# Samples and a norm row by DMA, and a new order from the out-projection to the up-projection

## The chip, the cores and the metric

The kernel runs on one core of a Trainium2 chip. The metric is the device time of one launch in microseconds. Of three runs of the kernel before, the median is 1061.47 us (1061.19 to 1062.1).

## What is computed

One layer of a hybrid decoder: 1,024 prompt tokens and 32 sample tokens (8 sequences of 4) of width 1,024, in float32.

```python
h = rms_norm(x, g_mix_pre) * (1 + sc1) + sh1
proj = h @ w_in
...
glu = a_c * jax.nn.sigmoid(b_c)
conv_c, new_cconv = causal_dwconv(glu, past_cconv, cconv_w)
y_c = jax.nn.silu(layer_norm(conv_c + cconv_b, cln_g, cln_b))
mix = jnp.concatenate([y_a, y_b, y_c], axis=-1) @ w_out
x = x + gt1 * rms_norm(mix, g_mix_post)

h = rms_norm(x, g_ffn_pre) * (1 + sc2) + sh2
up = h @ w_up
up_c, new_ffn = causal_dwconv(up, past_ffn, ffn_conv_w)
gate, val = jnp.split(up_c, 2, axis=-1)
ff = (jax.nn.silu(gate) * val) @ w_down
x = x + gt2 * rms_norm(ff, g_ffn_post)
```

`gate` and `val` have 2,816 columns each, 22 blocks of 128. A sample token's convolution takes the two last up-projected rows of its own sequence, so its 32 columns stand apart from the prompt's.

## The kernel before

Matmuls are made from two parts of each operand: a rounded one, `hi` (a cast on ACT), and the rest, `lo` (a subtraction on DVE, `sub_to`, L927). Three matmuls, hi by hi, hi by lo and lo by hi, make one product.

**Out-projection** (`mm2`, L833). Token tiles 0, 1 and 2 go first, together, with k-tiles in the order 2, 3, 4, 1, 0, 5, 6, 7; then tiles 3 to 8, tile 8 being the 32 samples. While k-tiles 3 and 4 run, the LayerNorm of the convolution's output is finished: `ln_rstd` (L442) makes 1,056 inverse deviations on POOL, three DMAs lay them as rows, three matmuls with K = 1 (`ln_bc`, L449) spread each third over the 128 partitions in PSUM, and `ln_apply` (L454, DVE) multiplies by them. `proj` (L607) is a small matmul of the pooling group; it takes its PSUM room from the same ring of two tiles (`psb`) as `ln_bc`. The w_out tiles `w` are loaded right behind the three row DMAs in SP's queue.

**From out-projection to up-projection.** Each token tile runs a chain: gate and residual (`gt`, `res`), second norm (`sq2`, `rs` on POOL, `xn2`), transposes on PE (`tr`, L897) and modulation (`mod`). The results of two neighbouring token tiles are combined into the operands of a scheme with seven products instead of eight (`t13`, `t24`, `t_hi`, `t_lo`).

**Up-projection** (`prod`, L1218). For each of 22 blocks of columns there are seven products (numbers 1 to 7) of 12 matmuls 128x512. Operands on the weights' side are the loaded `raw` and `rawb` and their sums (`s_sum`, `s_hi`, `s_lo`, tiles `s`, `sh`, `sl`). `snap` (ACT, L1223) copies a partial result from PSUM, and `c11`, `c22`, `c12`, `c21` (L1233, DVE, and L1239) add parts into `fext`, the convolution's input. Products 1 and 2 of blocks 0 and 1 run before tile 8 of the tokens is ready; then block 0 goes on with 6, 5, 7, 3, 4.

**Samples.** `smp` (L1253) multiplies the samples against each block, leaving them transposed in PSUM, in four parts. `smp_ev` copies this 128x128 with ACT (L1258); `smp_t` (L1262) turns it and adds pairs of parts on PE, by a matmul with the 0/1 matrix `sel`; `smp_out` (L1266, ACT) copies the result into `fext`.

**What sets the order.** PE, DVE, ACT and SP run in program order, and that order is written by hand: `at(time, f, args)` puts a call on a list, and `play` runs the list sorted by the time. The times serve the sorting alone; an instruction starts when its engine reaches it and its operands are there. Each block's operands are then taken from PSUM and the pools in that order, so that a wait in one place holds all behind it on the same engine.

Of the kernel before, what the change touches and what calls it, by code (L numbers as in the profile page):

```python
# [50 lines left out]
def body(ctx: ExitStack, tc: tile.TileContext, a, o):  # L51
# [17 lines left out]
    one1 = lnp.tile([P, P], F32, name="one1")  # L69
# [11 lines left out]
    dve.memset(one1, 1.0)  # L81
# [9 lines left out]
    gd = tc.dram_tile([9, 2048], F32, name="gd")  # L91

# [855 lines left out]
    def t24(i):  # L948
        r0, r1 = h2_of(i - 1), h2_of(i)
        sub_to(r1[:, 4:8], r1[:, 4:8], r0[:, 0:4])  # L950
        sub_to(r0[:, 4:8], r0[:, 4:8], r1[:, 4:8])

    def t_hi(i):
        act.copy(ycol(0, i), h2_of(i))

    def t_lo(i):
        sub_to(ycol(1, i), h2_of(i), ycol(0, i).bitcast(F32))
# [4 lines left out]
    def chain(i, e, tt):  # L962
        at(e, sq1, i)
        at(e + 1.1, rs, i)
        at(e + 1.2, gt, i)
        at(e + 2.4, res, i)
        at(e + 3.7, sq2, i)
        at(e + 4.8, rs, i)
        at(e + 5.5, xn2, i)
        at(tt, tr, i, 0)  # L970
        at(tt, tr, i, 1)
        at(tt + 0.7, mod, i, 0)
        at(tt + 1.1, mod, i, 1)
        at(tt + 2.5, h2_hi, i)
        if i % 2:
            at(tt + 2.5, t13, i)
            at(tt + 3.0, h2_lo, i)
            at(tt + 3.6, t24, i)
            for n, j in enumerate((i, i - 1)):
                at(tt + 4.6 + 1.1 * n, t_hi, j)  # L980
                at(tt + 5.7 + 1.2 * n, t_lo, j)
        else:
            at(tt + 3.5, h2_lo, i)

    def chain_s(e):
        for dt, f in ((0, sq1), (2.2, rs), (2.4, gt), (3.7, res), (4.9, sq2), (6.0, rs), (6.8, xn2)):
            at(e + dt, f, 8)
        for q in range(2):
            at(e + 11.74, tr, 8, q)
            at(e + 12.4 + 0.1 * q, mod, 8, q)  # L990
# [105 lines left out]
    for n, i in enumerate(order):  # L1096
# [7 lines left out]
        if i == 8:  # L1104
            at(t - 2.99, gate_s)
            chain_s(t + 2.0)
        else:
            te = max(t, te + 7.0)
            chain(i, te, te + 9.0)
# [3 lines left out]
    fs = {p: tc.dram_tile([FT // 2, P, 512], F32, name=f"fs{p}") for p in range(1, 8)}  # L1113
    U = {}
# [16 lines left out]
    def open_b():  # L1131
# [6 lines left out]
        U["sel"] = pools["p3b"].tile([P, 2, 32], F32, name="sel")  # L1138
        iv = ident.rearrange("p (a b n) -> p a b n", a=2, n=32)
        dve.tensor_tensor(out=U["sel"], in0=iv[:, :, 0], in1=iv[:, :, 1], op=ALU.add)  # L1140
# [25 lines left out]
    def s_sum(i, p):  # L1166
        ra, rb = U["ra", i], U["rb", i]
        a11, a12, a21, a22 = ra[:, 0:512], ra[:, 512:1024], rb[:, 0:512], rb[:, 512:1024]
        if p == 5:
            t, t2 = (pools["p3"].tile([P, 512], F32, name="s1", bufs=2) for _ in range(2))  # L1170
            U["s", i] = {5: t, 7: a21, 6: t2, 3: a12, 4: a22}
            dve.tensor_tensor(out=t, in0=a21, in1=a22, op=ALU.add)
        elif p == 7:
            sub_to(a21, a11, a21)
        elif p == 6:
            sub_to(U["s", i][6], U["s", i][5], a11)
        elif p == 3:
            sub_to(a12, a12, U["s", i][6])
# [30 lines left out]
    def prod(i, p):  # L1209
# [5 lines left out]
        for k in range(4):  # L1215
# [5 lines left out]
    def snap(i, n):  # L1221
        t = pools["p3" if n == "a" else "p3b"].tile([P, 512], F32, name=f"sn{n}", bufs=1)
        act.copy(t, x_of(i)[:, 0])  # L1223
        U["sn", n, i] = t
# [101 lines left out]
    DP, DS = 2.75, 1.6  # L1326
# [7 lines left out]
    at(t8 + 14.5, open_z)  # L1334
    at(t8 + 14.51, open_b)
    for i in range(2):
        t1 = t8 + 2 * DP * i
        at(t8 - 5.0 + 2.2 * i, a_hi, i)
        at(t8 - 3.9 + 2.2 * i, a_lo, i)
        at(t1, prod, i, 1)  # L1340
        at(t1 + DP, prod, i, 2)
        at(t1 + DP + 0.1, snap, i, "a")
        at(t8 + (6.1 if i == 0 else 14.6), c11, i)
# [9 lines left out]
    def sample(i, t, t1=None, t2=None):  # L1353
# [3 lines left out]
        at(t + DS, smp_ev, i)  # L1357
        at(t1 - 0.01, smp_t, i)
# [3 lines left out]
    for i in range(FT):  # L1362
        if i == 0:
            for p, ts, th, tl in ((5, 5.0, 6.1, 9.2), (6, 5.1, 6.0, 6.9), (7, 15.6, 15.7, 16.3), (3, 15.8, 16.8, 17.5), (4, 0, 12.0, 14.7)):
                if p != 4:
                    at(t8 + ts, s_sum, 0, p)
                at(t8 + th, s_hi, 0, p)
                at(t8 + tl, s_lo, 0, p)
            sample(0, b + DP + 0.9, b + 3 * DP + 2 * DS)
            sample(1, b + 2 * DP + DS + 0.9, b + 4 * DP + 2 * DS, b + 5 * DP + 2 * DS + 7.0)  # L1370
            seq = [(prod, 0, 6), (DS + 0.9,), (prod, 0, 5), (DS,), (prod, 0, 7), (prod, 0, 3), (prod, 0, 4)]
# [8 lines left out]
        for f, *args in seq:  # L1380
# [9 lines left out]
            j, p = args  # L1390
# [5 lines left out]
            elif p == 6:  # L1396
                at(done + (0 if j else 0.8), snap, j, "b")
            elif p == 5:
                at(done, snap, j, "c")
                if j:  # L1400
                    at(done + 0.8, c22, j)
            elif p == 7 and j == 0:
# [7 lines left out]
        if i == 0:  # L1410
            tg, tv = t - 1.0, t + 0.8
# [369 lines left out]
```

## Time and profile before

| | us |
|---|---|
| median of three runs | 1061.47 |
| the profiled execution | 1063.64 |
| its span | 1061.8 |
| PE busy | 1030.5 (97%) |
| DVE busy | 825.0 (78%) |
| ACT busy | 466.6 (44%) |
| POOL busy | 38.2 (4%) |

The profiled execution is 2.17 us above the median, and 1.84 us of it lie outside the span. TensorE's mean granted clock over it is 0.992 of full speed. The parts of the page go from the whole to the single instruction: busy shares of the engines, the span in slices, groups of instructions by line, DMA. A list of PE's waits tells which operand ended each, and a timeline gives start and length of single instructions. Matmuls overlap in the pipeline: a 128x512 is shown 0.39 us long while the next starts 0.23 us later, so distances are read from start to start.

### The profile page before, as it was taken

To read this page: it belongs to the slowest core of one execution; us is meant where nothing else is said; L and a number is where in the kernel's file an instruction comes from. 1 tells how busy PE (TensorE), PEld (TensorE's weight loads), DVE (VectorE), ACT (ScalarE), POOL (GpSimd) and SP (SyncE) were. 2 spreads that over 40 slices of the span, in tenths; PEclk is the share of its full clock that TensorE was granted. 3 is DMA by queue.
4 is the path that set the end of the run, shared out by engine and by line. 5 is a ranking of instruction groups with operands and counts; after the bars stand their busy time and mean duration, and the time that the engine had idled before them with its cause. 6 is when DMAs were issued, how large, how long until landed. Compare 5 with 4: busy or idle time off the path is not lost. (4 is left out here: it accounts for less than half of the span.)

```text
span 1061.8 us, 15512 instructions
## 1 busy us (share of the span) xinstructions
PE 1030.5 (97%) x6094; PEld 864.8 (81%) x6094; DVE 825.0 (78%) x1142; ACT 466.6 (44%) x835; POOL 38.2 (4%) x56
## 2 busy tenths in 40 slices
PE   5999999999999989999999999999999999999997
PEld 4999989997687668888888888888888787778885
DVE  5688898978547788888788788778878764987584
ACT  6331111115747745445454444544545464335551
POOL 3000000001011100000000000000000000020100
PEclk9999999999999989999999999999999999999999
DMA  8776652211512413323314223322323694325272
GB/s 334 262 228 194 193 185 88 63 41 17 184 43 99 156 54 99 109 64 127 110 60 129 91 79 115 104 80 92 114 74 110 228 412 179 109 73 161 90 267 100
DMA packets 68050, 141.10 MB, mean 133 GB/s; under 512 B 17156, under 2 KB 28676, under 8 KB 64904
## 3 DMA queue, kind: packets, MB, share of 16 engines
q1 hardware_dynamic: 66632, 135.77, 39.0%
q10 hardware_dynamic: 1344, 4.33, 1.0%
q8 instruction: 48, 0.79, 0.3%
q14 instruction: 26, 0.21, 0.1%
HBM read 110.18 MB, written 29.90 MB: 132 GB/s over the span
## 5 line engine op out<-in xcount | busy, mean ns | idle before, releaser
L1280 DVE SCALAR_TENSOR_TENSOR facc<-fext,par,facc 128x1072 f32<-128x1072 f32 x88 | 117.2, 1332 | 14.2 <-ACT facc L1273 12.7
L535 DVE SCALAR_TENSOR_TENSOR yb<-cext,par,yb 128x1024 f32<-128x1024 f32 x90 | 111.9, 1278 | 0.8
L279 PE MATMUL psa<-hh,whi 128*128 128x352 f32 x372 | 82.0, 328 | 0.0
L279 PE MATMUL psa<-hh,wlo 128*128 128x352 f32 x372 | 80.2, 323 | 0.0
L1532 PE MATMUL psd<-whi 128*128 128x512 f32 x204 | 80.1, 393 | 0.0
L279 PE MATMUL psa<-hl,whi 128*128 128x352 f32 x372 | 80.1, 323 | 0.0
L1532 PE MATMUL psd<-whi,wlo 128*128 128x512 f32 x204 | 79.6, 390 | 0.1
L1532 PE MATMUL psd<-wlo,whi 128*128 128x512 f32 x204 | 79.5, 390 | 0.1
L1513 ACT CAST whi<-fa 128x512 fp32r<-128x512 f32 x73 | 45.3, 621 | 70.9 <-PE psb L1532 24.6
L927 DVE TENSOR_TENSOR wlo<-fa,whi 128x512 fp32r<-128x512 f32 x73 | 49.9, 684 | 31.0 <-ACT whi L1513 31.0
L1218 PE MATMUL psc<-hh,sh 128*128 128x512 f32 x176 | 69.7, 396 | 2.8 <-DVE fext L1233 2.8
L1218 PE MATMUL psb<-hh,sh 128*128 128x512 f32 x176 | 71.3, 405 | 0.0
L1218 PE MATMUL psc<-hl,sh 128*128 128x512 f32 x176 | 69.6, 396 | 0.9 <-DVE hl L927 0.9
L1218 PE MATMUL psc<-hh,sl 128*128 128x512 f32 x176 | 69.4, 395 | 0.0
L1218 PE MATMUL psb<-hh,sl 128*128 128x512 f32 x176 | 68.8, 391 | 0.0
L1218 PE MATMUL psc<-bh,whi 128*128 128x512 f32 x176 | 68.6, 390 | 0.0
L1218 PE MATMUL psc<-bh,wlo 128*128 128x512 f32 x176 | 68.5, 389 | 0.0
L1218 PE MATMUL psc<-bl,whi 128*128 128x512 f32 x176 | 68.5, 389 | 0.0
L1218 PE MATMUL psb<-hl,sh 128*128 128x512 f32 x176 | 68.5, 389 | 0.0
L279 PEld LDWEIGHTS psa<-hh,whi 128*128 128x128 f32 x372 | 62.8, 189 | 6.4 <-issue 4.1
L279 PEld LDWEIGHTS psa<-hh,wlo 128*128 128x128 f32 x372 | 63.8, 188 | 0.0
L279 PEld LDWEIGHTS psa<-hl,whi 128*128 128x128 f32 x372 | 63.1, 188 | 0.0
(270 smaller groups left out, 2318.0 us busy)
## 6 DMA issues: line engine op xcount, KB each, us to landing
fa<-fs SPq DMA_DIRECT2D x73, 256.0 KB, 3.8
adaw<-in_ada SPq DMA_DIRECT2D x16, 1024.0 KB, 7.5
raw<-in_w_up SPq DMA_DIRECT2D x22, 512.0 KB, 3.6
rawb<-in_w_up SPq DMA_DIRECT2D x22, 512.0 KB, 3.7
fs<-facc SPq DMA_DIRECT2D x44, 256.0 KB, 2.5
b<-in_w_down SPq DMA_DIRECT2D x18, 512.0 KB, 7.3
fs<-whi SPq DMA_DIRECT2D x33, 256.0 KB, 2.3
adaw<-in_adag SPq DMA_DIRECT2D x8, 1024.0 KB, 7.1
```

Of the source, the lines that this page charges most:

```text
L279: pe.matmul(ps[:, c, 0:CW], lhsT=wt[:, k, :], rhs=h[:, k, c * CW:(c + 1) * CW], start=(k == 0 and n == 0), stop=(k == KT - 1 and n == 2))
L535: dve.scalar_tensor_tensor(out=y[:, 0:NPR], in0=e[:, k:k + NPR], scalar=par[:, off + k:off + k + 1], in1=y[:, 0:NPR], op0=ALU.mult, op1=AL ...
L927: dve.tensor_tensor(out=out, in0=x, in1=y, op=ALU.subtract)
L1218: pe.matmul(out, lhsT=w[:, ks], rhs=h(k), start=(p in (1, 2, 7) and k == 0 and n == 0), stop=(k == 3 and n == 2), skip_group_check=True)
L1280: dve.scalar_tensor_tensor(out=acc[:, 0:1072], in0=e[:, k:k + 1072], scalar=par[:, wo + k:wo + k + 1], in1=acc[:, 0:1072], op0=ALU.mult, o ...
L1513: act.copy(hi[:, 0:512], R[n, "raw"])
L1532: pe.matmul(ps, lhsT=s[:, cs], rhs=w, start=(first and m == 0), stop=(j == HK - 1 and m == 2), skip_group_check=True)
```

## The change

There are three parts.

1. **Norm row.** `ln_bc`, its matrix of ones and the three row DMAs go. `ln_rstd` stores the 1,056 values to DRAM (`rsd`) by one DMA, and a second DMA reads them back to all 128 partitions (540 KB) into a `zc` tile; `ln_apply` multiplies by that tile instead of by PSUM.
2. **Samples.** `smp_t` and `sel` go. `smp_ev` becomes a DVE transpose of 32x32 parts from PSUM, with a DMA that stores the 64 KB to DRAM (`smpd`). `smp_ld` is new: four DMAs of 32 partitions by 4 by 32 values (512 pieces of 128 bytes in all) bring it back as `smq`. `smp_out` becomes a DVE addition of two parts of 32 columns. This holds for all 22 blocks.
3. **The transition.** Tables `FIRST`, `SECOND` and `THIRD` fix the order of the last token tiles' chains and block 0's weights. Block 0's products run 6, 7, 5 (three of four k), then tile 8's transposes, the last k of 5, both samples' `smp`, 3, 4. `t24` falls into `t2` and `t4`, `t_hi` and `t_lo` into halves. Some results get other rooms: `t2` of tile 7, the sums 7 and 3 of block 0, one `snap` and tile 8's transposes. The weights of the blocks after are loaded and split at other times.

The core of the diff:

```diff
 def ln_rstd():
...
         pool.tensor_tensor(out=rt, in0=vt, in1=nhalf[0:96, :], op=ALU.pow)
-        for c in range(3):
-            sync.dma_start(rows[32 * c:32 * c + 1, :], rt[32 * c:32 * c + 32, :])
-
-    def ln_bc(c):
-        rw = slice(32 * c, 32 * c + 1)
-        ln["r", c] = psb()
-        pe.matmul(ln["r", c][:, 0:CW], lhsT=one1[rw, :], rhs=rows[rw, :], start=True, stop=True,
-                  tile_position=(32 * c, 0))
+        sync.dma_start(rsd.rearrange("o (q n) -> (o q) n", n=11), rt)
+        ln["r"] = zc_tile()[:, 0:T]
+        sync.dma_start(ln["r"], rsd.broadcast_to([P, T]))
...
     def tr(i, q):
         rows = tile_rows(i)
-        pt = psb()
-        pv = pt.rearrange("p (k n) -> p k n", n=P)[:, :, 0:rows]
+        if i < 8:
+            pv = psb().rearrange("p (k n) -> p k n", n=P)
+        else:
+            pv = U["s"][:, 256 + P * q:256 + P * q + P].rearrange("p (k n) -> p k n", n=rows)
...
-    def t24(i):
...
+    def t2(i):
         r0, r1 = h2_of(i - 1), h2_of(i)
+        st[i, "t2"] = r1[:, 4:8] if i < 7 else st[i, "t"][:, 0:512].rearrange("p (k n) -> p k n", n=P)
+        sub_to(st[i, "t2"], r1[:, 4:8], r0[:, 0:4])
+
+    def t4(i):
+        r0 = h2_of(i - 1)
+        sub_to(r0[:, 4:8], r0[:, 4:8], st[i, "t2"])
...
+    def t_hi(i, r=slice(0, KT)):
+        act.copy(ycol(0, i)[:, r], t_src(i, r))
...
+        elif p == 7 and i == 0:
+            t = U["s", i][7] = stream.tile([P, 1024], F32R, name="whi").bitcast(F32)[:, 0:512]
+            sub_to(t, a11, a21)
...
-    def prod(i, p):
+    def prod(i, p, k0=0, k1=4):
...
     def smp_ev(i):
         t = pools["p3"].tile([P, P], F32, name="smp", bufs=2)
-        act.copy(t, U["s"][:, P * (i % 2):P * (i % 2) + P])
-        U["smp", i] = t
-
-    def smp_t(i):
-        pe.matmul(U["s"][:, 256:320], lhsT=U["smp", i], rhs=U["sel"].rearrange("p a n -> p (a n)"), start=True, stop=True)
+        dve.transpose(out=t, in_=U["s"][:, P * (i % 2):P * (i % 2) + P])
+        sync.dma_start(smpd[i], t)
+
+    def smp_ld(i):
+        u = U["smp", i] = pools["p3"].tile([P, P], F32, name="smq", bufs=2)
+        for j in range(4):
+            sync.dma_start(u[32 * j:32 * j + 32].rearrange("m (q t) -> m q t", t=32),
+                           smpd[i].rearrange("(q m) (j t) -> j m q t", q=4, j=4)[j])
 
     def smp_out(i, v):
-        e = e_of(i, v)
-        act.copy(ext_parts(e, 2)[2], U["s"][:, 256 + 32 * v:288 + 32 * v].rearrange("p (s t) -> p s t", t=ST))
+        e, u = e_of(i, v), U["smp", i].rearrange("p (q s t) -> p q s t", q=4, t=ST)
+        dve.tensor_tensor(out=ext_parts(e, 2)[2], in0=u[:, 2 * v], in1=u[:, 2 * v + 1], op=ALU.add)
         act.copy(ext_state(e, 2), U["fst"][:, i + FT * v, 1:9, :])
...
+    FIRST = [(s_sum, 0, 5), (t2, 7), (s_sum, 0, 6), (t_hi, 7, HI), (s_hi, 0, 6), (t_lo, 7, HI), (snap, 0, "a"), (s_lo, 0, 6),
+             (c11, 0), (s_sum, 0, 7), (t_hi, 7, LO), (s_hi, 0, 7), (t_lo, 7, LO), (s_lo, 0, 7), (gt, 8), (res, 8), (t_hi, 6, LO),
...
+    for n, (f, *args) in enumerate(FIRST):
+        at(b - 0.5 + 0.01 * n, f, *args)
...
         at(t, smp, i)
-        at(t + DS, smp_ev, i)
-        at(t1 - 0.01, smp_t, i)
+        if i:
+            at(t + DS + 0.05, smp_ev, i)
+        at(t + DS + 4.0, smp_ld, i)
         at(t1 + 0.6, smp_out, i, 0)
...
-            seq = [(prod, 0, 6), (DS + 0.9,), (prod, 0, 5), (DS,), (prod, 0, 7), (prod, 0, 3), (prod, 0, 4)]
+            seq = [(prod, 0, 6), (prod, 0, 7), (prod, 0, 5, 0, 3), (2 * DS,), (prod, 0, 3), (prod, 0, 4)]
+            at(b + 2.8 * DP, prod, 0, 5, 3, 4)
```

**DVE, around the first addition into `fext` (`c11` of block 0).** Here `px` are the tokens' operands, `s`, `sl` the weights' sums and their lo parts. Before:

```order
270 L1172 TENSOR_TENSOR s_3394<-rawb 128x512
271 L927 TENSOR_TENSOR s_3395<-s_3394,raw 128x512
272 L927 TENSOR_TENSOR bl<-px,bh 128x4x128
273 L882 SCALAR_TENSOR_TENSOR px<-px,rs 32x1024
274 L927 TENSOR_TENSOR px<-px 128x512 x2
275 L1233 TENSOR_TENSOR fext_3343<-psc,sna 128x4x128
276 L927 TENSOR_TENSOR sl<-s_3395,sh 128x512
277 L927 TENSOR_TENSOR hl<-px,hh 128x8x128
```

After:

```order
268 L1173 TENSOR_TENSOR s_3411<-rawb 128x512
269 L923 TENSOR_TENSOR pt<-px 128x512
270 L923 TENSOR_TENSOR s_3412<-s_3411,raw 128x512
271 L923 TENSOR_TENSOR hl<-pt,hh 128x4x128
272 L923 TENSOR_TENSOR sl<-s_3412,sh 128x512
273 L1243 TENSOR_TENSOR fext_3335<-psc,sna 128x4x128
274 L923 TENSOR_TENSOR whi<-raw,rawb 128x512
275 L923 TENSOR_TENSOR hl<-px,hh 128x4x128
276 L923 TENSOR_TENSOR sl<-whi,sh 128x512
```

The addition into `fext` no longer stands behind the scaling of tile 8 (the 32x1024 row), nor behind the two `px` subtractions after it; of those only the one into `pt` is left ahead, and one half of `hl` with it. Tile 8's own steps come later.

**SP's queue, from the first `rawb` loads to the second block of weights.** Before:

```order
57 L1151 DMA rawb<-in_w_up 128x1024 x2
58 L1137 DMA fst<-in_st_f 128x792
59 L1147 DMA raw<-in_w_up 128x1024
60 L1151 DMA rawb<-in_w_up 128x1024
61 L1147 DMA raw<-in_w_up 128x1024
```

After:

```order
59 L1141 DMA fst<-in_st_f 128x792
60 L1270 DMA smpd<-smp 128x128 x2
61 L1152 DMA rawb<-in_w_up 128x1024
62 L1148 DMA raw<-in_w_up 128x1024
63 L1275 DMA smq<-smpd 32x4x32 x8
64 L1148 DMA raw<-in_w_up 128x1024
65 L1270 DMA smpd<-smp 128x128
```

Stores and loads of the samples now stand between the weights' loads: two stores, then a `rawb` and a `raw` of 512 KB each, then the eight loads of `smq` of blocks 0 and 1.

**DVE, ahead of `c21` of block 0** (the addition of `psb` and `snb`, which empties the PSUM tile that product 7 of block 1 writes next). Before:

```order
297 L1233 TENSOR_TENSOR fext_3487<-psb,snc 128x4x128
298 L927 TENSOR_TENSOR sl<-s_3573,sh 128x512
299 L927 TENSOR_TENSOR sl<-rawb,sh 128x512
300 L927 TENSOR_TENSOR wlo<-raw,whi 128x1024
301 L927 TENSOR_TENSOR sl<-s_3572,sh 128x512
302 L1233 TENSOR_TENSOR fext_3487<-psb,snb 128x4x128
303 L1280 SCALAR_TENSOR_TENSOR facc<-fext_3343,par,facc 128x1072 x2
```

After:

```order
300 L923 TENSOR_TENSOR raw<-raw,s_3582 128x512
301 L923 TENSOR_TENSOR sl<-s_3582,sh 128x512
302 L923 TENSOR_TENSOR sl<-rawb,sh 128x512
303 L923 TENSOR_TENSOR sl<-s_3581,sh 128x512
304 L1280 TENSOR_TENSOR fext_3335<-smq 128x8x4
305 L1280 TENSOR_TENSOR fext_3555<-smq 128x8x4
306 L1243 TENSOR_TENSOR fext_3555<-psb,snb 128x4x128
```

The two additions from `smq` (L1280), which wait for DMAs, now stand ahead of the addition of `psb` and `snb` (L1243, L1233 before); before, nothing that waits for a DMA stood there.

## Rows read from the trace of the kernel before

**Rows 1.** The profile's part 1: busy time, share of the span, instructions, by engine.

```profile
...
PE 1030.5 (97%) x6094; PEld 864.8 (81%) x6094; DVE 825.0 (78%) x1142; ACT 466.6 (44%) x835; POOL 38.2 (4%) x56
...
```

**Rows 2.** PE's waits: tile and line that waited, releaser: total us, times, longest.

```profile
...
PE psc L1218 <- DVE fext L1233: 2.8, 1, 2.8
...
PE psb L607 <- DVE yb L454: 2.2, 1, 2.2
...
PE psc L1218 <- DVE hl L927: 0.9, 1, 0.9
...
```

**Rows 3.** PE's timeline, 380 to 396: start, us, line, names [idle before <-releaser].

```profile
...
380.55 0.39 PE L1218 MATMUL psc<-bh,whi 128*128 128x512 f32 x1
...
383.05 0.39 PE L1218 MATMUL psc<-bh,wlo 128*128 128x512 f32 x1
386.19 0.76 PE L1218 MATMUL psc<-hh,sh 128*128 128x512 f32 x1 [2.75 <-DVE fext L1233]
...
392.26 0.63 PE L1218 MATMUL psc<-hh,sl 128*128 128x512 f32 x1
...
394.01 0.78 PE L1253 MATMUL psb<-raw,hs 128*32 128x128 f32 x3 [0.51 <-PE psb L897]
...
395.49 0.53 PE L1218 MATMUL psc<-hh,sh 128*128 128x512 f32 x1
...
```

**Rows 4.** Windows: us, busy of PE, PEld, DVE, ACT, POOL, PEclk, DMA share, GB/s.

```profile
...
383.30:395.50 12.20, 7.97 (x54) 5.32 (x53) 9.26 (x17) 4.83 (x7) 0.73 (x3) 0.72 0.12 29
387.00:392.00 5.00, 4.17 (x10) 3.34 (x11) 3.48 (x5) 2.04 (x3) 0.63 (x2) 0.50 0.00 0
440.00:460.30 20.30, 20.30 (x119) 16.72 (x118) 16.92 (x25) 9.63 (x19) 0.00 (x0) 1.00 0.33 109
262.50:278.00 15.50, 13.28 (x44) 8.43 (x43) 8.32 (x10) 7.81 (x11) 0.00 (x0) 0.89 0.53 131
...
```

**Rows 5.** DVE's timeline, 382 to 394, columns as in rows 3.

```profile
...
382.71 1.27 DVE L882 SCALAR_TENSOR_TENSOR px<-px,rs 32x1024 f32<-32x1024 f32 x1
384.02 1.42 DVE L927 TENSOR_TENSOR px<-px 128x512 f32<-128x512 f32 x2
385.36 0.68 DVE L1233 TENSOR_TENSOR fext<-psc,sna 128x512 f32<-128x512 f32 x1
...
393.29 0.29 DVE L917 TENSOR_TENSOR hs<-psb,aT 128x128 f32<-128x128 f32 x1 [2.03 <-PE psb L897]
...
```

**Rows 6.** PE's timeline around the samples of two later blocks.

```profile
...
410.83 0.39 PE L1218 MATMUL psc<-hh,sl 128*128 128x512 f32 x1
411.15 0.30 PE L1253 MATMUL psb<-raw,hs 128*32 128x128 f32 x2
...
431.13 0.39 PE L1218 MATMUL psc<-hh,sl 128*128 128x512 f32 x1
431.36 0.33 PE L1262 MATMUL psb<-sel,smp 128*128 128x64 f32 x2
431.62 0.30 PE L1253 MATMUL psb<-raw,hs 128*32 128x128 f32 x2
...
```

**Rows 7.** PE's timeline in the out-projection, around the first norm matmul.

```profile
...
262.60 0.85 PE L449 MATMUL psb<-row,one 1*128 1x352 f32 x2
263.38 0.73 PE L833 MATMUL psc<-whi,y0h 128*128 128x512 f32 x2
...
```

**Rows 8.** ACT's timeline in the same stretch.

```profile
...
268.46 1.05 ACT L792 CAST rh<-w 128x1024 fp32r<-128x1024 f32 x1 [5.33 <-DMA w<-in_w_out]
...
```

**Rows 9.** DMA issues: names, engine, op, xcount, KB each, median us to landing.

```profile
...
rawb<-in_w_up SPq DMA_DIRECT2D x22, 512.0 KB, 3.7
...
G<-gd SPq DMA_DIRECT2D x2, 512.0 KB, 5.3
...
x1d<-px ACTq DMA_DIRECT2D x1, 128.0 KB, 1.9
...
row<-rt SPq DMA_DIRECT2D x3, 1.4 KB, 1.7
...
```

More of the change, by code (lines that the diff above doesn't have):

```diff
@@ L946, in t13, with t_src, t_lo @@
         sub_to(r1[:, 0:4], r1[:, 4:8], r1[:, 0:4])
-    def t24(i):
+    def t2(i):
         r0, r1 = h2_of(i - 1), h2_of(i)
[L950 to L957, printed above, removed]
+        st[i, "t2"] = r1[:, 4:8] if i < 7 else st[i, "t"][:, 0:512].rearrange("p (k n) -> p k n", n=P)
[3 more added lines that the diff above has]
+        sub_to(r0[:, 4:8], r0[:, 4:8], st[i, "t2"])
+    def t_src(i, r):
+        return h2_of(i)[:, r] if i < 7 or r.start == 0 else st[i, "t2"]
+    def t_hi(i, r=slice(0, KT)):
+        act.copy(ycol(0, i)[:, r], t_src(i, r))
+    def t_lo(i, r=slice(0, KT)):
+        sub_to(ycol(1, i)[:, r], t_src(i, r), ycol(0, i)[:, r].bitcast(F32))
     def gate_s():
@@ L973, in chain @@
         at(tt + 1.1, mod, i, 1)
+        if i == 7:
+            at(tt + 2.5, t13, i)
+            return tt
         at(tt + 2.5, h2_hi, i)
@@ L985, in chain_s @@
     def chain_s(e):
-        for dt, f in ((0, sq1), (2.2, rs), (2.4, gt), (3.7, res), (4.9, sq2), (6.0, rs), (6.8, xn2)):
+        for dt, f in ((0, sq1), (2.2, rs)):
             at(e + dt, f, 8)
-        for q in range(2):
-            at(e + 11.74, tr, 8, q)
-            at(e + 12.4 + 0.1 * q, mod, 8, q)
     load(16)
@@ L1108, in body @@
             te = max(t, te + 7.0)
-            chain(i, te, te + 9.0)
+            tt7 = chain(i, te, te + 9.0)
     t8 = t
     fs = {p: tc.dram_tile([FT // 2, P, 512], F32, name=f"fs{p}") for p in range(1, 8)}
+    smpd = tc.dram_tile([FT, P, P], F32, name="smpd")
     U = {}
@@ L1137, in open_b @@
         sync.dma_start(U["fst"], a["st_f"])
-        U["sel"] = pools["p3b"].tile([P, 2, 32], F32, name="sel")
-        iv = ident.rearrange("p (a b n) -> p a b n", a=2, n=32)
-        dve.tensor_tensor(out=U["sel"], in0=iv[:, :, 0], in1=iv[:, :, 1], op=ALU.add)
     p3_cm = tc.tile_pool(name="p3", bufs=1, reuse_waits="tile")
@@ L1176, in s_sum @@
             sub_to(U["s", i][6], U["s", i][5], a11)
+        elif p == 3 and i == 0:
+            t = U["s", i][3] = stream.tile([P, 1024], F32R, name="whi").bitcast(F32)[:, 0:512]
+            sub_to(t, a12, U["s", i][6])
         elif p == 3:
@@ L1214, in prod @@
         out = four(ps)
-        for k in range(4):
+        for k in range(k0, k1):
             ks = slice(P * k, P * k + P)
@@ L1221, in snap @@
     def snap(i, n):
-        t = pools["p3" if n == "a" else "p3b"].tile([P, 512], F32, name=f"sn{n}", bufs=1)
+        if n == "c" and i == 0:
+            t = stream.tile([P, 1024], F32R, name="wlo").bitcast(F32)[:, 0:512]
+        else:
+            t = pools["p3b" if n == "c" else "p3"].tile([P, 512], F32, name=f"sn{n}", bufs=1)
         act.copy(t, x_of(i)[:, 0])
@@ L1338, in body @@
         at(t8 - 5.0 + 2.2 * i, a_hi, i)
-        at(t8 - 3.9 + 2.2 * i, a_lo, i)
+        at(t8 - 3.9 + 5.0 * i, a_lo, i)
         at(t1, prod, i, 1)
         at(t1 + DP, prod, i, 2)
-        at(t1 + DP + 0.1, snap, i, "a")
-        at(t8 + (6.1 if i == 0 else 14.6), c11, i)
+    for n, (f, *args) in enumerate(FIRST):
+        at(b - 0.5 + 0.01 * n, f, *args)
+    for n, (f, *args) in enumerate(SECOND):
+        at(b + DP + 0.2 + 0.01 * n, f, *args)
+    at(b + 2.75 * DP, tr, 8, 0)
+    at(b + 2.75 * DP, tr, 8, 1)
+    at(b + 2.75 * DP, mod, 8, 0)
+    at(b + 2.75 * DP, mod, 8, 1)
+    for n, (f, *args) in enumerate(THIRD):
+        at(b + 3 * DP + DS + 0.01 + 0.01 * n, f, *args)
     def weights(i, t):
@@ L1363, in body @@
         if i == 0:
[L1364 to L1370, printed above, removed]
-            seq = [(prod, 0, 6), (DS + 0.9,), (prod, 0, 5), (DS,), (prod, 0, 7), (prod, 0, 3), (prod, 0, 4)]
+            sample(0, b + 3 * DP, b + 5 * DP + 2 * DS - 0.6, b + 5 * DP + 2 * DS + 0.1)
+            sample(1, b + 3 * DP + DS, b + 5 * DP + 2 * DS + 3.0, b + 5 * DP + 2 * DS + 7.0)
+            seq = [(prod, 0, 6), (prod, 0, 7), (prod, 0, 5, 0, 3), (2 * DS,), (prod, 0, 3), (prod, 0, 4)]
+            at(b + 2.8 * DP, prod, 0, 5, 3, 4)
         elif i == FT - 2:
@@ L1389, in body @@
             t += DP
-            j, p = args
+            j, p = args[:2]
             done = t + 0.1
@@ L1396, in body @@
             elif p == 6:
-                at(done + (0 if j else 0.8), snap, j, "b")
-            elif p == 5:
+                at(done, snap, j, "b")
+            elif p == 5 and j:
                 at(done, snap, j, "c")
-                if j:
-                    at(done + 0.8, c22, j)
-            elif p == 7 and j == 0:
                 at(done + 0.8, c22, j)
```

30 lines of the change are left out of this document (16 added, 14 removed).

## The prediction

> **What bounds the kernel now.** I began with the busy shares: PE works for 1030.5 of 1061.8 us [rows 1], so about 31 us can be had by closing its gaps, and the rest only by taking work off it. Next came the list of PE's waits. One matter is large and close by the change: 2.8 us for an addition into `fext` and 0.9 for a `hl` [rows 2]. The timeline puts them at the first product of block 0 after the tokens' last tile. The last matmul of the product ahead starts at 383.05 and the next one at 386.19, and the twelve matmuls of that product run to 392.26 [rows 3]. In between the granted clock is 0.50, the lower of the two levels (1.2 GHz of 2.4); over the whole stretch from 383.3 to 395.5 it is 0.72, with PE busy for 7.97 of 12.20 us [rows 4]. So the gap costs more than the wait: it also halves the clock behind it. In a later block PE is full for all of 20.30 us, and DVE has 16.92, ACT 9.63 [rows 4]. There PE alone sets the time, and only work taken from PE counts. The third place is the out-projection between 262.5 and 278: PE 13.28 of 15.50, clock 0.89 [rows 4], with a wait of 2.2 us for `yb` [rows 2].
>
> **The transition.** Why did the addition come late? DVE does the scaling of tile 8 at 382.71 and two `px` subtractions until 385.4, and only then, at 385.36, the addition [rows 5]. The change puts the addition ahead of tile 8's scaling and leaves one of those two subtractions before it, with half a `hl`. Counted with DVE's own lengths (0.68 for 128x512, the new ones included), it ends near 382, and the `hl` half for product 6 earlier still. PE then goes on at 383.05 + 0.23 = 383.28 without a wait. What this takes away, by start to start:
> - The wait: 386.19 - 383.28 = 2.91 us [rows 3].
> - The slow product. From 386.19 to 392.26 are eleven steps and the `hl` wait; with a last step of 0.43 it took 6.50. At the full clock eleven steps took 383.05 - 380.55 = 2.50 [rows 3], so a product is 2.73. The difference is 3.77.
> - 0.51 us between tile 8's transposes and the samples at 394.01 [rows 3], and about 0.6 for transposes and samples at the lower clock or on the way up. This 0.6 is an estimate (bounds 0 and 0.9), from 392.26 to 395.49 less what the same takes later.
> - Against it stands a new wait of about 0.4: the samples' matmuls come right behind the last quarter of product 5, and DVE's four `hs` steps of 0.29 [rows 5] need 1.2 us after the transposes, where that quarter gives PE 0.7.
>
> Sum: -2.91 - 3.77 - 0.51 - 0.6 + 0.4 = **-7.4**. Products 7 and 5 have operands that DVE finishes 1 to 2 us before PE comes; tile 8's second norm is the tightest with about 0.6 us to spare, POOL's step in it included. If that is used up, PE waits for the overrun alone; if a gap of over 2 us returns, the clock goes with it. Range -4.5 to -8.0.
>
> **What is late next: the samples' way through DRAM.** PE would reach block 1's product 7 at 383.3 + 3 x 2.73 + 0.7 (transposes) + 0.4 + two samples of 1.2 (an estimate, under the 1.48 from 394.01 to 395.49 at a clock that rises [rows 3]) + three products of 2.73 + one sample = about 404.4. That product needs the PSUM tile that `c21` of block 0 empties, and on DVE `c21` now stands behind the two `smp_out` of block 0, which wait for four DMAs. These two are about 0.2 each, `c21` 0.68, so the data must be there by 403.3. The store leaves at about 395.3, when the first sample is done and transposed. A store of 128 KB lands in 1.9, three tiny ones with short rows in 1.7 [rows 9]; so the loads are issued from 397.2, some 0.4 apart on SP's queue, the fourth at 398.8. If nothing is in their way they land at 400.7: no cost. If they go behind the `rawb` and `raw` that are issued just ahead (each 512 KB, 3.7 us [rows 9]), it is 398.8 + 3.7 + 1.7 = 404.2, and PE waits 0.9. Behind that wait stand `c21`, the first taps of block 0 (ACT waits for `fext` too) and block 1's later sums; I add 0.6 for small waits of products 5 and 4 of block 1. I take **+1.5**, nearer the late end, as the big loads stand ahead in the same queue; range 0 to +4.
> By the Trainium skill (DMA: Bandwidth & Descriptors, Specifications) pieces under 512 B are below what gives line rate, since the DMA engine then reads and writes back; each `smq` load is made of 128-byte pieces. The page gives no price for one such load; the row with 44-byte pieces, 96 of them, landed in 1.7 and speaks against a large one, but 512 at once stand in no row. What it would do if it held is the first rival.
>
> **The samples on PE.** In a later block the last matmul of a product starts at 431.13, `smp_t` at 431.36, and the samples at 431.62: 0.49. Where no `smp_t` stands between, the same takes 410.83 to 411.15: 0.32 [rows 6]. So each costs PE 0.17, and there are 22: **-3.7**. The bounds are 0.17 x 20 = 3.4, and 0.26 (its own step) x 22 = 5.7. PE is full there, so all of it counts. DVE gets a transpose in place of ACT's copy, and two additions of 32 columns; none stands in the trace, the nearest are the 0.29 of a 128x128 from PSUM [rows 5] and about 0.2 for a narrow step. That is 0.7 on 16.92 of 20.1 us: covered. SP gets five more issues per block; at 0.4 each they are 2 us of a queue that is not on the path. In later blocks some five products, 5 x 2.73 = 13.6 us, lie between a block's samples and the place where `smp_out` stands, against about 7.5 for transpose, store, issues and loads (1.9, 1.6, 3.7 and what lies between).
>
> **The norm row.** Three `ln_bc` leave PE; the first stands at 262.60 and the next matmul at 263.38 [rows 7], so 0.78 each, 2.3 in all. They also leave the ring of two PSUM tiles, so the first `proj` doesn't wait for `yb` any more; the 2.2 of [rows 2] is not gone though, it moves. The third `proj` needs a room that ACT empties, and ACT is held at its casts of `w`, of which the first waits 5.33 us for its DMA, to 268.46 [rows 8]. In SP's queue these loads now stand behind the broadcast of 540 KB; one of 512 KB took 5.3 alone, where the three row DMAs took 1.7 [rows 9]. I expect the `w` tiles 1.3 to 3.3 us later, and PE with a gap of 3 to 4 us at 270 to 274, lower clock after it as before. Bounds: a gain of 2.3 if the loads aren't delayed, a loss of 1 if they are by the whole 3.3, since the ring's gain and the removed matmuls cover all but that. What is won here is also cut later by the casts of k-tile 7, which ACT reaches in its own time. I take the middle, **-1.2** (the mean of -2.3 and 0, for a delay that eats part).
>
> **Sum:** -7.4 + 1.5 - 3.7 - 1.2 = -10.8. The profiled execution took 1063.64, 2.17 above the median of 1061.47, so it would come to 1052.8 and the median to **1050.7**. The terms' ends add up to -8.0 + 0 - 5.7 - 2.3 = -16.0 on one side and -4.5 + 4 - 3.4 + 1 = -2.9 on the other, 1045.5 and 1058.6; since not all ends come at once, this case's own range is 1047 to 1056.
>
> **The rivals.**
> - *The samples hold DVE longer* (0.20). The `smq` loads of small pieces land some 3 us later than my late end, at 407. Then PE waits 3 to 4 us before product 7 of block 1, and as with the gap of 2.75 us, the clock halves behind it for a product: 2 to 3 us more. For: eight loads of the kind at once, behind 1 MB. Against: the 1.7 us of the row DMAs. Sum: -7.4 + 6 - 3.7 - 1.2 = -6.3, or 1055.2.
> - *The gap stays* (0.08). The chain to product 6 or 7 is longer than I counted (a `sl` or a `hl` half, a POOL step of the second norm), PE waits over 2 us somewhere in block 0 and runs at the lower clock after it. Against: in the rows DVE has the operands 1 us early. Then the transition gives -2, and the sum is -5.4: 1056.1.
> - *Slower: DVE waits in every block* (0.09). DVE runs in order, so a `smp_out` whose `smq` isn't there holds all behind it. In later blocks DVE has 20.1 - 17.6 = 2.5 us to spare. If the loads come so late that DVE stands for more than that, PE loses the rest in each of about 20 blocks. It decides from 2.5 + 10.8 / 20 = 3.0 us of standing per block: then the kernel is as slow as before. At 4 us the loss is 1.5 x 20 = 30, and the time 1081. That needs store and loads to take 13.6 + 3 us after the samples. The rows give 7.5, and other loads in flight (DMA share 0.33 in such a block [rows 4]) could double it, not more.
>
> **How the numbers follow.** My forecast has 0.63, the rivals 0.20, 0.08 and 0.09. The likeliest time is 1050.7. The range from 1046.5 to 1057.5 leaves out the third rival and the ends. About 0.2% (2.1 us) is what a measurement of this kernel can tell from no change. Faster: 0.62 of my case, all of the first rival but 0.02, most of the second: 0.86. Same: 0.05. Slower: 0.09.
>
> **What would show it.** In the trace after: PE's wait for `fext` before product 6 of block 0 is gone, the clock between 383 and 395 is near 1.00, and product 6 of block 1 starts at about 400.5, as the sum of steps above has it. A new wait of PE before product 7 of block 1, released by DVE, is 0 to 2 us long; DVE's own list shows a wait for `smq`. Later blocks are 0.17 us shorter each, and DVE never waits for `smq` in them. In the out-projection `w` lands later than 268.46. The prediction is wrong if PE shows waits for DVE in blocks after the second, or a stretch of clock 0.50 after 400.

## The result and the profile after

| | before | after |
|---|---|---|
| median of four runs, us | 1061.78 | 1049.90 |
| range | 1061.19 to 1062.19 | 1048.60 to 1051.97 |
| profiled execution, and its span | 1063.64, 1061.8 | 1051.97, 1050.2 |

The ratio is 0.9891, with a 95% interval of 0.9875 to 0.9907: 11.9 us less, where 10.8 less, 1050.7 us, was forecast. A second set of runs beside the kernel before gave 1048.64 us and 0.9880 (0.9867 to 0.9893).

The page's first part, after (busy us, share, instructions):

```profile
PE 1021.5 (97%) x6044; PEld 855.4 (81%) x6044; DVE 828.7 (79%) x1208; ACT 458.3 (44%) x771; POOL 37.7 (4%) x56
```

PE is still the bound; it is busy for 9.0 us less than in [rows 1]. PE's waits, after (us in total, times, longest), without those that both kernels have:

```profile
PE psc L827 <- ACT hh L686: 1.5, 1, 1.5
...
PE psb L1225 <- DVE fext L1243: 0.7, 1, 0.7
...
PE psc L1225 <- DVE fext L1243: 0.4, 1, 0.4
...
```

All three rows of [rows 2] are gone: 2.8 for `fext`, 2.2 for `yb`, 0.9 for `hl`. What came in their place is smaller. PE's timeline, after (start, length, line, names):

```profile
382.17 0.39 PE L1225 MATMUL psc<-bh,wlo 128*128 128x512 f32 x1
382.40 0.39 PE L1225 MATMUL psc<-hh,sh 128*128 128x512 f32 x1
...
391.82 0.62 PE L1263 MATMUL psb<-raw,hs 128*32 128x128 f32 x3 [0.28 <-DVE hs L913]
...
399.59 0.39 PE L1225 MATMUL psc<-hh,sh 128*128 128x512 f32 x1
...
404.13 0.47 PE L1225 MATMUL psb<-hh,sh 128*128 128x512 f32 x1 [0.65 <-DVE fext L1243]
```

Product 6 of block 0 (382.40) follows the product ahead by one step of 0.23, where [rows 3] has 383.05 and 386.19. Block 1's product 6 begins at 399.59, 17.19 us later; in the kernel before the same way, from 383.28 (one step of 0.23 behind the 383.05) to 408.34, took 25.06. Then comes the new wait of 0.65. Windows of the same trace (us, busy of PE, PEld, DVE, ACT, POOL, clock, DMA share, GB/s):

```profile
382.40:399.59 17.19, 16.91 (x133) 13.49 (x132) 15.71 (x29) 8.49 (x16) 0.73 (x3) 1.00 0.22 65
262.50:280.00 17.50, 16.69 (x71) 12.75 (x69) 11.81 (x12) 10.20 (x14) 0.00 (x0) 1.00 0.69 151
500.00:520.30 20.30, 20.30 (x118) 16.50 (x116) 17.49 (x27) 9.46 (x15) 0.00 (x0) 1.00 0.40 123
```

Where [rows 4] has clocks of 0.72 and 0.89, both stretches now have 1.00. A later block leaves PE full as before, and DVE has 17.49 of 20.3.

**Where the time went, by marks in the two traces.** The first matmul of the out-projection stands at 256.30 before and 259.81 after: 3.51 later. From it to block 0's first product: 115.18 and 110.79, so -4.39. From there to block 1's product 6: 36.86 and 28.99, -7.87. From there to the down-projection's first matmul: 423.89 and 421.83, -2.06. The rest: 229.57 and 228.78, -0.79. These sum to -11.6, the difference of the spans. The first entry has nothing to do with the change's places, so I began with it.

### The profile page after: what moved, and what is told of

The parts are those of the page before. It is cut to its first block, busy times and chain, and to the rows that moved or that the text cites. A ratio compares the mean times of both kernels' runs of the same rounds, so it can differ in the third digit from the quotient of the medians.

```text
span 1050.2 us, 15560 instructions
## 1 busy us (share of the span) xinstructions
PE 1021.5 (97%) x6044; PEld 855.4 (81%) x6044; DVE 828.7 (79%) x1208; ACT 458.3 (44%) x771; POOL 37.7 (4%) x56
## 5 line engine op out<-in xcount | busy, mean ns | idle before, releaser
L1294 DVE SCALAR_TENSOR_TENSOR facc<-fext,par,facc 128x1072 f32<-128x1072 f32 x88 | 117.2, 1332 | 15.4 <-ACT facc L1287 13.9
L1287 ACT ACTIVATE facc<-fext,par 128x1072 f32<-128x1072 f32 x44 | 52.6, 1195 | 26.1 <-DVE fext L1243 22.6
```

Of the source, the lines that this page charges most:

```text
L1287: act.activation(acc[:, 0:1072], e[:, 2:1074], AF.Copy, scale=par[:, wo + 2:wo + 3])
L1294: dve.scalar_tensor_tensor(out=acc[:, 0:1072], in0=e[:, k:k + 1072], scalar=par[:, wo + k:wo + k + 1], in1=acc[:, 0:1072], op0=ALU.mult, o ...
```

## The experiments

"The changed kernel" is the one of the result. A median stands beside the runs of the kernel before on the same chip; their medians went from 1060.30 to 1061.78, and most kernels' runs spread over 0.9 to 4.4 us, so differences of 1 us between two medians say little, and I lean on the traces there. `r_after`, `a_ln_old`, `b_smp_pe` and `d_old_order` are one set on one chip, so their medians compare best; `c_ln_only`, `l_dummy`, `f_np_late` and `h_w_first` are a second set, the rest a third. Each kernel has one profiled execution, the changed kernel two (the result's and r_after's).

### The late start: r_after

The changed kernel without an edit.

> The changed kernel once more, to see whether its late start is its own. In the first profile of it an input tile xt landed late, PE waited 1.9 us at 21.4 us and had a granted clock of 0.94 up to 30 us, and the out-projection began 3.5 us later than before. Theory (chance of the DMA): the start is as before in this profile, PE's second wait for xt 0.2 us or less, the span near 1046.8, and the transition (first matmul of product 6 of block 0) starts near 379.0. Rival (the change moves the start): the wait of about 1.9 us comes again, span near 1050.

It gave 1048.64 us; the profiled execution's span is 1046.4, 3.8 below the first profile's. PE's longest wait for the input after its first one, in the first profile of the changed kernel, then in this one:

```profile
21.42 3.40 PE L233 MATMUL psx<-ident,xt 128*128 128x128 f32 x16 [1.92 <-DVE xt L222]
```

```profile
19.78 1.06 PE L233 MATMUL psx<-ident,xt 128*128 128x128 f32 x8 [1.83 <-DVE xt L222]
```

The theory was half right. The waits of that kind came again (1.83 in one, and 11.1 us for `xt` in all), so they are not a rarity. But from that wait's end to the next kind of work it is 2.25 us here (19.78 to 22.03) and 3.32 in the first profile (21.42 to 24.74), where the granted clock was 0.50 from 22 to 25 (here 1.00), and the out-projection begins at 256.95, 0.65 later than before, not 3.51. Profiles of the other kernels here show such waits of 0 to 1.4 us. So some 2.9 us of the first profile belong to that execution and not to the change, and against this one the difference of the spans is 15.4 us, not 11.6.

### The norm row: a_ln_old, c_ln_only, l_dummy

Undone in the changed kernel (a), and done alone in the kernel before (c):

```diff
-        sync.dma_start(ln["r"], rsd.broadcast_to([P, T]))
+        for c in range(3):
+            sync.dma_start(rows[32 * c:32 * c + 1, :], rt[32 * c:32 * c + 32, :])
...
+                at(t, ln_bc, i)
                 at(t + 3.0, ln_apply, i)
```

> The changed kernel with the norm row as before: three row DMAs, three matmuls that spread it (K = 1), multiplication from PSUM. Theory by the traces: the norm row gave 4.4 us (its three matmuls 3.0, the wait of 2.2 for yb, the lower clock after it 1.5, less 1.5 to 2.3 that come back as a wait for hh), so this is 4.4 slower than the changed kernel, about 1053 to 1054. Rival, the prediction's own figure: 1.2 slower, about 1050 to 1051.

> The kernel before with the norm row by DMA alone. Undoing that part in the changed kernel cost 2.45 us; its trace had a wait of 1.5 for yb and no lower clock after it, where the trace of before had 2.2 and a clock of 0.50 to 0.69. Theory (what the part gives depends on that wait): alone it gives 2.4 on the median if the runs of before mostly have the short wait, up to 4.7 if they have the long one; the trace shows no wait for yb, a wait of about 1.5 for hh, and a clock of 1.00 from 262 to 280. Rival (the prediction's step): w lands 1.3 to 3.3 us later behind the broadcast of 528 KB, PE stands 3 to 4 us at the third proj, and the gain is about 1.2.

Undone, it is 1051.09 against 1048.64 of the changed kernel, 2.45 slower; alone, 1058.74 against 1061.48 (ratio 0.9976, 0.9967 to 0.9985), 2.7 faster. The two agree, between the prediction's 1.2 and the 4.4 of the marks. The reason stands in one row, PE's wait for `yb` with the part undone:

```profile
272.76 0.86 PE L607 MATMUL psb<-w,pw 128*128 128x352 f32 x2 [1.51 <-DVE yb L454]
```

It is 1.51 here, and 2.2 in [rows 2]. Behind the 2.2 the clock fell (0.89 over the stretch, [rows 4]); behind the 1.51 it is 1.00 throughout, and the way from the first out-projection matmul to block 0's first product takes 112.97 instead of 115.18. The changed kernel's two profiles have 110.79 and 110.52 there. So the part gives 2.2 to 2.5 against an execution with the short wait and 4.4 to 4.7 against one with the long one. The kernel before was profiled in a long one.

Then the matmuls alone, put back with nobody reading their result:

```diff
+            pe.matmul(psb()[:, 0:CW], lhsT=one1[rw, :], rhs=rows[rw, :], start=True, stop=True,
+                      tile_position=(32 * c, 0))
```

> The changed kernel with the three K = 1 matmuls put back in their places, writing a PSUM tile that nobody reads (rows of other content); the norm row still comes by DMA. It takes the price of the three matmuls apart from the ring's. Theory: PE loses 3 x 0.99 = 3.0 ahead of k-tile 4 and gets about 1.5 back, as the wait for hh behind it (1.48) goes: 1.5 slower than the changed kernel. Rival (nothing is absorbed): 3.0 slower.

It took 1049.47, 0.8 above r_after, but in a set in which the kernel before was 0.75 slower too. By its marks the stretch is 111.24, between 0.4 and 0.7 longer than the changed kernel's two (110.79 and 110.52). PE's wait of 1.5 for the out-projection's `hh` is gone from its list of waits. The 3 us of the matmuls are thus mostly paid back by waits behind them. The rival (nothing absorbed) falls, and the theory's 1.5 was too much as well. The stretch of a_ln_old (112.97) is 1.73 longer than this one: that is what the ring's rooms and the old way of the row cost, with the wait of 1.51 in it.

### The queue to w: h_w_first, f_np_late

First the `w` loads ahead of the broadcast alone, then ahead of the store of the pooling state too:

```diff
     at(0.0, w_load, 1)
+    at(0.0, ln_load)
```

```diff
-        sync.dma_start(o["n_p"][p], ext_new(u, PP))
...
     at(0.0, w_load, 1)
+    at(0.0, pool_st, 0)
```

In the second, both `w` loads came out ahead of the broadcast as well: SP's order is not all written by hand, as that of PE, DVE and ACT is, though the section on the kernel before says so. Nor does `w` stand right behind the row DMAs there: the pooling store (258.37) stands between them, as it does after the change.

> The changed kernel with the w loads ahead of the norm's broadcast in SP's queue, but behind the store of the pooling state as before. Prediction's step (the broadcast holds w by 1.3 to 3.3 us): w lands that much earlier here than in the changed kernel. Theory by the traces (the broadcast isn't in w's way, the small pieces are): w lands within 0.7 us of the changed kernel's, and the time is within 0.7 us of it.

> The changed kernel with SP's queue in another order: the two w_out loads w right behind the store of the norm row, then the broadcast, then the store of the pooling state (1152 pieces of 60 bytes). Theory: w waits for these small pieces, not for bytes; w lands 3 us or more earlier than in the changed kernel (10.9 us behind the first out-projection matmul there), ACT's chain to hh starts earlier and the wait of 1.5 for hh goes, unless the later broadcast holds the first multiplication by the norm: 0 to 1.5 faster. Rival: the queue isn't what w waits for; w lands the same and nothing moves.

ACT's first cast of `w`, in r_after, in h_w_first and in f_np_late (in the last its row holds both casts):

```profile
267.87 1.05 ACT L786 CAST rh<-w 128x1024 fp32r<-128x1024 f32 x1 [4.08 <-DMA w<-in_w_out]
```

```profile
265.79 1.05 ACT L788 CAST rh<-w 128x1024 fp32r<-128x1024 f32 x1 [2.85 <-DMA w<-in_w_out]
```

```profile
262.53 2.00 ACT L788 CAST rh<-w 128x1024 fp32r<-128x1024 f32 x2
```

Counted from the first out-projection matmul (256.95, 256.11, 255.79) that is 10.92, 9.68 and 6.74; in the kernel before, 268.46 - 256.30 = 12.16. With the broadcast behind it, `w` is there 1.2 us earlier, so the theory written for h_w_first (within 0.7) misses the time. But the 540 KB are not what holds it, as SP's queue shows, first in r_after, then in h_w_first:

```profile
257.02 0.33 SPq L442 DMA_DIRECT2D rsd<-rt  x1
258.42 0.33 SPq L444 DMA_DIRECT2D zc<-rsd  x1
259.49 1.10 SPq L779 DMA_DIRECT2D w<-in_w_out  x2
```

```profile
257.24 1.14 SPq L781 DMA_DIRECT2D w<-in_w_out  x2
```

The broadcast (`zc`) is issued 1.40 behind the store that it reads from (`rsd`, which lands in 1.4 by the page), and SP stands for 1.07 of that; all behind it stands too. So `w` is issued 2.54 behind the out-projection's first matmul in r_after and 1.13 in h_w_first. From its issue to ACT's cast it is 8.38 with the broadcast in front and 8.55 without, the pooling store in front in both; over the nine executions here with the broadcast in front it is 7.6 to 9.0. In the kernel before, the issues of the three row DMAs take SP 1.91, `w` is issued at 259.06, 2.76 behind the mark, and the cast comes 9.40 later (8.67 in a_ln_old). So the change did not make `w` later: the stand for the store takes the place of the row DMAs' issues.

The pooling store in front costs 2.9 or more, 0.6 of it for its issue: in f_np_late `w` is issued 0.50 behind the mark, and ACT finds it ready. That is what the theory of f_np_late has, and its rival falls. With only the broadcast moved behind `w`, PE has another wait, of 2.0 for DVE's `rl`, which stands behind a wait of DVE for the norm:

```profile
268.81 1.26 DVE L450 TENSOR_TENSOR yb<-yb,zc 128x1056 f32<-128x1056 f32 x1 [3.94 <-DMA zc<-rsd]
```

So h_w_first gains nothing (1049.91), and f_np_late is at 1046.44 us (ratio 0.9864, 0.9844 to 0.9884). Its stretch takes 108.26, 2.3 less than r_after's and more than the theory's 1.5, and neither `yb` nor the out-projection's `hh` is in its list of waits. By the medians of two sets it is 2.2 below the changed kernel; the intervals overlap, and the stretch in the traces is the firmer ground. f_and_e below has the same edit and repeats it, with 108.30.

### The transition: d_old_order, t_c11_short, t_c11_long

The kernel before with the other two parts, so that only the transition is the old one:

> The kernel before with the norm row and the samples by DMA, and the old order of the transition (products 6, 5, 7, 3, 4; chains and weights as before). Theory: the transition is worth 7.4 us by itself, so the gap of 2.75 us before product 6 and the granted clock of 0.5 behind it are there, and this is 7 to 8 us slower than the changed kernel, about 1056.5. Rival: the parts are worth less or more together; if the samples by DMA cost more in the old order (block 0's smp_out comes after product 7 in it, and waits for DMAs) it is above 1058.

It took 1054.41, so the transition is worth 5.8 us net, less than the theory's 7 to 8; the rival (above 1058) falls too. Its rows, PE's first steps of product 6, then the window behind them:

```profile
382.44 0.47 PE L1209 MATMUL psc<-hh,sh 128*128 128x512 f32 x1 [2.76 <-DVE fext L1224]
384.08 0.62 PE L1209 MATMUL psc<-hl,sh 128*128 128x512 f32 x1 [1.17 <-DVE hl L921]
```

```profile
382.00:388.00 6.00, 4.38 (x11) 3.31 (x12) 4.74 (x7) 3.24 (x6) 0.64 (x2) 0.72 0.06 12
```

The gap of 2.76 is there, and the clock again falls behind it, but later than in the kernel before and for less time: its steps of 0.43 begin at 384.50 and end at 387.83, where the 0.50 of [rows 4] lasts to the product's end at 392. The product takes 5.85 instead of 6.50. c_ln_only, also with the old order, has the same: a gap of 2.76, then 5.76 for the product.

With c_ln_only and b_smp_pe (below) there are four kernels, all with the new norm row, that have the old or the new order and the samples on PE or by DMA. From block 0's first product to the down-projection's first matmul they take, in one profiled execution each (two for the changed kernel), in us:

| | samples on PE | samples by DMA |
|---|---|---|
| old order | 459.96 (c_ln_only) | 455.69 (d_old_order) |
| new order | 453.95 (b_smp_pe) | 450.13 and 450.82 (the changed kernel) |

So the transition gives 6.0 where no sample goes by DMA, and 5.6 or 4.9 where they do; the samples by DMA give 4.3 in the old order, which has no new wait with them, and 3.8 or 3.1 in the new one. The 0.5 to 1.1 between these is what the samples' DMAs cost in the new order. The kernel before took 460.75, 0.8 more than c_ln_only, and its longer stretch at the lower clock is in that.

Then one step of the transition was turned back in two sizes: `c11` of block 0 later on DVE.

```diff
-             (c11, 0), (s_sum, 0, 7), (t_hi, 7, LO), (s_hi, 0, 7), (t_lo, 7, LO), (s_lo, 0, 7), (gt, 8), (res, 8), (t_hi, 6, LO),
+             (s_sum, 0, 7), (t_hi, 7, LO), (s_hi, 0, 7), (t_lo, 7, LO), (s_lo, 0, 7), (gt, 8), (c11, 0), (res, 8), (t_hi, 6, LO),
```

(t_c11_long; t_c11_short has `c11` ahead of the gate.)

> The changed kernel with the first addition into fext (c11 of block 0) moved on DVE behind the three steps for product 7 (a sum, a half of hl, a sl: 2.06 us in the changed kernel's trace). PE reached product 6 with 0.47 us to spare; now it should wait 1.6 us for fext. Theory (a wait of this length leaves the clock alone, as those of 1.2 to 1.5 did): the granted clock behind it stays 1.00, and as waits behind it (hs 0.3, fext 0.2 to 0.7) shrink, the run is 0.7 to 1.5 slower than the changed kernel. Rival (any gap here halves the clock): product 6 takes 5 to 6.5 us instead of 2.73 and the run is 4 slower.

> As the run before, with c11 also behind the gate of tile 8 (32x1024, 1.22 us): PE should wait 2.9 us for fext, as in the kernel before. Theory of the prediction (the wait is paid once and the clock behind it once more): the granted clock falls to about 0.5, product 6 takes 5 to 6.5 us instead of 2.73, and the run is 4 to 6 slower than the changed kernel, which is most of what the whole transition gave. Rival (the lower clock came from something else in the old order): the clock stays 1.00 and the run is 2 to 2.9 slower.

Their waits came out shorter than I had counted, since DVE reached `c11` earlier: 0.55 us and

```profile
381.28 0.47 PE L1225 MATMUL psc<-hh,sh 128*128 128x512 f32 x1 [1.96 <-DVE fext L1243]
```

with a clock of 1.00 behind both. The short one is at 1049.15, 0.5 above the changed kernel, and its rival (any gap halves the clock) falls. By its marks the long one's profiled execution is 2.6 behind r_after's (452.73 against 450.13). The long one's six runs go from 1049.05 to 1055.59, median 1052.09; the profiled one was 1050.71. A wait of 1.96 that leaves the clock alone explains the fast end. The slow end would fit a fall of the clock behind it in some executions, but no profile of such a one exists, 6.5 us is more than the 2 to 3 us that the fall cost elsewhere, and the mean granted clocks of the six runs (0.993 to 0.997) do not follow their times: the run of 1053.12 has 0.996, as the profiled one has. The cause stays open. The experiment did not reach the 2.9 us that it was made for; d_old_order is the one that shows the price of that.

### The samples: b_smp_pe, e_smq_first, f_and_e

> The changed kernel with the samples turned by PE as before (matmul with sel, ACT copies, no DRAM), everything else kept. Theory: 22 x 0.17 = 3.7 come back on PE, 20 of them in full blocks; the wait of 0.65 before product 7 of block 1 and about 0.4 behind it go. Net 2.5 slower than the changed kernel. Rival: the store and loads cost more than shown, since DVE's queue is held 2.3 us; then the two are equal or this one is faster.

With the samples turned on PE as before, everything else kept:

```diff
-        at(t + DS + 4.0, smp_ld, i)
+        at(t1 - 0.01, smp_t, i)
```

(with the old `smp_ev`, `smp_t`, `smp_out`), 1051.61, 3.0 slower. From one block's samples to the next it is 20.46 in this kernel and in the kernel before, and 20.27 or 20.28 in r_after: 0.19 in each of 18 blocks, without an exception. The new waits of the changed kernel take the rest back.

In the changed kernel DVE waits for `smq`, and `c21` stands right behind it, at 403.30; below are the row of that wait, and the landing of two of the new DMAs on the page (names, KB each, median us). The stores `smpd` of 64 KB land in 1.5.

```profile
403.09 0.29 DVE L1280 TENSOR_TENSOR fext<-smq 128x32 f32<-128x32 f32 x2 [2.31 <-DMA smq<-smpd]
```

```profile
smq<-smpd SPq DMA_DIRECT2D x88, 16.0 KB, 1.9
...
zc<-rsd SPq DMA_DIRECT2D x1, 528.0 KB, 5.3
```

The loads of 128-byte pieces land in 1.9 us, 4.1 at most; by the prediction's count they are no cost with nothing in front of them. To see that, they went ahead of block 2's weights:

```diff
-        at(t + DS + 4.0, smp_ld, i)
+        at(t + DS + (4.0 if i else 1.5), smp_ld, i)
```

> The changed kernel with the four smq loads of block 0 ahead of the rawb and raw of block 2 in SP's queue (there they stood behind). Prediction's step (the queue behind 1 MB makes smq late): DVE's wait of 2.3 us for smq goes, and PE's wait of 0.2 to 0.7 before product 7 of block 1 with it; 0.2 to 0.7 faster, if raw of block 2, now issued some 2.5 us later, still lands before its samples. Rival: raw is late then, PE waits before the samples of block 2, and the run is 0 to 2 slower.

> The changed kernel with both orders of SP's queue: the w loads ahead of the broadcast and the pooling store (alone 2.2 faster than the changed kernel), and the smq loads of block 0 ahead of block 2's weights. Theory: the two places are 100 us apart, so their gains add: 2 to 3 faster than the changed kernel, about 1046. Rival: the second one costs what it gives, and this is equal to the first alone or up to 2 slower.

DVE's wait for `smq` is gone, and so is PE's for `fext`. In its place PE waits for the weights that were put behind:

```profile
400.55 0.30 PE L1263 MATMUL psb<-raw,hs 128*32 128x128 f32 x2 [2.00 <-DMA raw<-in_w_up]
```

1050.01 us, not better than the changed kernel; the rival holds. f_and_e has the same wait (1.9) and 1047.66, while f_np_late alone has 1046.44. So loading the samples first gains nothing: what DVE no longer waits for them, PE waits for the weights. f_np_late has the lowest median here.

## Why the prediction was right, and where not

The time was forecast within 0.8 us, the gain within 1.1 to 1.3, and the terms show how much of this was earned.

- **The transition, -7.4.** Right in its mechanism, too large in size. Between block 0's first product and block 1's product 6 the trace gave -7.87 against the kernel before, of which 2 x 0.19 belong to the samples' matmuls: -7.5. The wait at product 6 is gone and the clock is 1.00; the new wait for `hs` is 0.28 where 0.4 stood; block 1's product 6 was forecast at 400.5 and stands at 399.59 in a trace that runs 0.9 us ahead. But the term was read from one execution of the kernel before, 2.17 us above its median, with a long stretch at the lower clock. In c_ln_only and d_old_order, where the same gap came again, the product behind it cost 0.7 less, and by the table above the transition is worth 6.0.
- **The samples' way through DRAM, +1.5.** Right in place and cause, a bit too much. The smq loads stand behind `rawb` and `raw`, DVE waits 2.31, PE 0.65 before block 1's product 7 (0.24 in r_after) and 0.4 once more; by the table it is 0.5 to 1.1. That the big loads in front are the cause is shown by e_smq_first.
- **The samples on PE, -3.7.** 0.19 instead of 0.17 per block: about -4.2 for 22, and 4.3 by the table. With the waits, the 423.89 us after the transition fell by 2.06, where -3.4 + 1.5 = -1.9 was counted. DVE's cover held: transposes take 0.31 each (22 in 6.8 us, by the page), `smp_out` 0.19, and no block after the second waits for `smq`.
- **The norm row, -1.2.** This step was wrong. It said that `w` lands 1.3 to 3.3 us later than before behind the bytes of the broadcast, so that PE gets a gap of 3 to 4 us and a lower clock. Those bytes held `w` by nothing that shows (8.38 from issue to cast with them in front, 8.55 without), and SP's stand for the store took no longer than the issues of the three row DMAs. The step had taken the difference of two landings (5.3 and 1.7) for the delay of what is queued behind: `w` was issued 2.54 behind the out-projection's start instead of 2.76, and cast at 10.92 instead of 12.16. PE met no such gap, and the clock stayed up. The matmuls were put too low as well: with the slower steps around them one costs 0.98 (262.05 to 263.95 in the trace before, less two steps of 0.46), not 0.78. The part gave 2.4 to 2.7 by the medians. Why `w` needs 9.40 from issue to cast in the kernel before and 7.6 to 9.0 in the others was not found.
- **The sum.** By the table and the medians of the norm row it would be -6.0 + 0.8 - 4.3 - 2.5 = -12.0; the medians moved by 11.9 and 12.1. Two executions of the changed kernel differ by 0.7 on the way that the table measures, so this is an estimate to about 1 us. Undoing one part at a time gives less, 5.8 + 3.0 + 2.45 = 11.2, as the new waits go with either of the first two. So the closeness of the forecast is part luck: the norm row, the samples and their way were forecast 2.6 too small in gain together, and the transition 1.4 too large.

Of the rivals, the one with the samples' loads landing at 407 didn't come: they landed at 403.1 in a trace that runs 0.9 us ahead of the one before. Neither did the gap stay, nor does DVE wait in every block. The Trainium skill (DMA: Bandwidth & Descriptors, Specifications) puts pieces under 512 B below line rate. The traces agree with that for both kinds of piece: 67.5 KB in 60-byte pieces took 8.7 us to land and 16 KB in 128-byte pieces 1.9, where 512 KB of `raw` took 3.6. That the DMA engine then reads and writes back, as it says, no run here shows. What such a DMA cost was decided by the queue: the pooling store by `w` behind it, the samples' loads by the 1 MB in front of them.

## What to carry to other kernels

A gap on TensorE is priced by what follows it too: in this kernel the 2.75 us ahead of one product cost another 2 to 3 us by the lower clock (6.50 - 2.73 - 0.88 = 2.9 before, 5.85 - 2.73 - 1.17 = 2.0 in d_old_order), while behind gaps of 1.5 (a_ln_old, r_after) and up to 2.0 (t_c11_long, e_smq_first) the clock stayed at 1.00. So look first for the gaps that the lower clock follows, and read them in more than one execution: behind the same gap of 2.75 the product took 6.50 in one and 5.76 and 5.85 in two others. Then move what the gap waits for, here one step on DVE, ahead of work that nobody waits for yet. When work leaves the bounding engine by way of DMAs, read the queue that they join: a small store or a bulk load in front of them, and what in turn stands behind, decide what the move costs. A load that reads what a store has just written makes its queue stand until the store has landed (1.07 us on SP here), and everything behind it.

## What the runs showed that I had not expected

- Waits of nearly the same length stand on either side of the clock's fall: behind 2.2 us for `yb` before it fell (0.89 over the stretch), behind 1.51 in a_ln_old, 1.96 in t_c11_long and 2.00 in e_smq_first it stayed at 1.00 in the profiled executions. Whether the length decides or the moment, these runs don't show. The six runs of t_c11_long spread over 6.5 us, those of the other kernels over 0.9 to 4.4.
- 1152 pieces of 60 bytes (67.5 KB) took 8.7 us to land, more than 528 KB of the norm's broadcast (5.3), and `w`, queued behind them, came later by 2.9 us or more.
- Three us of matmuls put back on the bounding engine (l_dummy) made its stretch 0.4 to 0.7 us longer: a share of 97% doesn't say that each stretch is bound by it.
